# A Hymba layer on one core: the second token block's first weight pair and three of its token factors kept in DRAM instead of being divided again

## The chip, the core and the metric

The program runs on one core of a Trainium2 chip. The metric is the device time of one execution in microseconds (us), lower is better. In single precision each operand of a product is divided into a high part (rounded to the matmul's format) and a low part (the rest), and three matmuls, high by high, high by low and low by high, stand for one product. This division, called a split below, is what the change is about.

## The reference, cut to what matters

```python
def swiglu(h, w_gate, w_up, w_down):
    a = jax.nn.silu(jnp.einsum('bld,df->blf', h, w_gate)) * jnp.einsum('bld,df->blf', h, w_up)
    return jnp.einsum('blf,fd->bld', a, w_down)

def reference(x, meta_tokens, ...):
    h = layer_norm(jnp.concatenate([meta, x], axis=1), ln_in_g, ln_in_b)
    for l in range(DEPTH):                    # DEPTH = 1
        mix = hybrid_mixer(h, ...)            # sliding-window attention beside gated linear attention
        h = layer_norm(ALPHA * h + mix, ln1_g[l], ln1_b[l])
        ffn = swiglu(h, w_ffn_gate[l], w_ffn_up[l], w_ffn_down[l])
        h = layer_norm(ALPHA * h + ffn, ln2_g[l], ln2_b[l])
    return h[:, N_META:]
```

2048 tokens, width 1024, hidden width 2816, float32. The change lies in `swiglu`, in the two products with the gate and up weights.

## The kernel before

The mixer stands in the first part of the span; the first gate product follows at about 965 us, the down product at about 1822 us.

**Gate and up.** The tokens are cut into two blocks of 1024 (`tb` 0 and 1), the 2816 hidden columns into eleven pairs of 256 (`p` 0 to 10). For each block and pair the 2 by 2 by 2 block product is done with seven products in place of eight (Strassen's scheme in Winograd's form). In the order of the program they are named after their token factor: b11, t2, t1, b21, t3, t4, b22. b11, b21 and b22 are plain quarters of the tokens (a quarter is 512 rows of the width by 512 tokens), t1 to t4 are sums and differences of quarters, kept in DRAM as `t_sc`. The weight factors are, in the same order, pa11, ps2, ps1, pa12, ps3, pa22, ps4: pa are plain quarters of the weights, ps sums and differences. A product is two halves of twelve matmuls, 128x128 by 512 columns: four slices of the width (k 0 to 3), three matmuls each.

**Token factors** are made once for a block (`make`): a quarter comes from DRAM in four rows of 256 KB (`r_b`, `r_t`, in a ring of four buffers, tag `cb`), and `split_into` writes the high part on ScalarE (ACT) and the low part on VectorE (DVE) or GpSimd (POOL) in turn (`h_b`, `h_t`). In the last pair of block 0 the code calls `make` for block 1 behind each product, since each factor has one buffer, which comes free with that product.

**Weight factors** are made anew for each pair and block (`weights`): four quarters of 512 KB are fetched about a pair ahead (`fetch_weights`, tiles `a11` to `a22`), POOL forms three of the sums and differences in `s1`, `a21`, `a11` and a fourth in `a12`, ACT writes the seven high parts, POOL four of the low parts (pa11, ps2, pa12, pa22) and DVE three (ps1, ps3, ps4). The divided factors (high and low, 1 MB) stand in a ring of four buffers, tag `whl`; the buffer of a factor comes free when the product four places earlier is done.

**Behind the products** DVE adds the seven results to the quarters of gate and up (`u`, `p`, `c`), ACT takes a tanh, DVE finishes the gates (`sa`, `sb`), POOL forms the factors of the down product (`sc`, `s4`), and seven stores of 256 KB a pair take them to DRAM (`a_sc`, `a_last`).

**What sets the order.** Each engine runs its instructions in the order in which the program was built; the builder's scheduler sets it from priorities and its own estimate of times, but what is marked `held` keeps the order in which it was written among its like. All loads and stores here go through one queue, that of SyncE (SP), in program order: an instruction there that waits for a buffer holds up everything behind it. DMA completions are counted on eight semaphores taken in turn, so that an issue also waits for the DMA eight places before it.

Of the kernel before, what the change touches and what calls it, by code (L numbers as in the profile page):

```python
# [20 lines left out]
NP = NF // 2  # L21
# [102 lines left out]
def body(ctx, tc, t, seq):  # L124
    nc = tc.nc
    NSB = seq // TB
    PSUM = bass.MemoryType.PSUM
    r32 = lambda ap: ap.bitcast(F32)

    cp = ctx.enter_context(tc.tile_pool(name="cp", bufs=1))  # L130
    dr = ctx.enter_context(tc.tile_pool(name="dr", bufs=1, space=bass.MemoryType.DRAM))
# [4 lines left out]
    HT = TF // 2  # L136
    NTB = seq // TF
# [46 lines left out]
    def split_into(hi, lo, src, lo_eng=None, hold=lambda i: i):  # L184
        hold(nc.scalar.activation(hi, src, AF.Copy))  # L185
        hold((lo_eng or nc.vector).tensor_tensor(lo, src, r32(hi), op=ALU.subtract))  # L186
# [547 lines left out]
    pools = {}  # L734

    def quarter(tb, kh, th, k, n):

        c = tb * TF + th * HT
        k0 = kh * (KT // 2) + k
        return n_scT[c // TB][:, k0 : k0 + n, c % TB : c % TB + HT]  # L740
# [37 lines left out]
        yield  # L778

    SOURCE = {"b11": (0, 0), "b21": (1, 0), "b22": (1, 1)}  # L780
    COMBINED = {"t2": (0, 0), "t1": (0, 1), "t4": (1, 0), "t3": (1, 1)}

    def make(f, tb):

        if f in FIRST:
            x = hb.tile([P, 2, KT // 2, HT], F32R, tag="h16", name=f"h_{f}_{tb}", bufs=2)
        else:
            pool = pools["hop1" if f in EARLY else "hop3" if f == "b22" else "hop2"]
            x = pool.tile([P, 2, KT // 2, HT], F32R, tag=f"h_{f}", name=f"h_{f}_{tb}", bufs=1)
        if f in FIRST and tb == 0:  # L790
            for k in range(0, KT // 2, 2):
                raw = staging(f"r_{f}{tb}_{k}").rearrange("p (k q) -> p k q", q=HT)
                if f in SOURCE:
                    nc.sync.dma_start(raw, quarter(tb, *SOURCE[f], k, 2))
                else:
                    i, j = COMBINED[f]
                    nc.sync.dma_start(raw, t_sc[tb][i, :, k : k + 2, j])
                split_into(x[:, 0, k : k + 2], x[:, 1, k : k + 2], raw, nc.vector)
            return x
        for k in range(KT // 2):  # L800
            if tb > 0:
                raw = pools["hop4"].tile([P, HT], F32, tag="cb", name=f"r_{f}{tb}_{k}", bufs=4)
            else:
                raw = pools["hop1"].tile([P, HT], F32, tag="mk", name=f"r_{f}{tb}_{k}", bufs=3)
            if f in SOURCE:
                row_ = nc.sync.dma_start(raw, quarter(tb, *SOURCE[f], k, 1)[:, 0, :])
            else:
                i, j = COMBINED[f]
                row_ = nc.sync.dma_start(raw, t_sc[tb][i, :, k, j])
            if tb > 0:  # L810
                tc.keep_in_program_order(row_)
            split_into(x[:, 0, k], x[:, 1, k], raw, nc.vector if k % 2 else nc.gpsimd)
        return x
# [695 lines left out]

    hops2 = ctx.enter_context(ExitStack())  # L1510
    c2 = ctx.enter_context(ExitStack())
    quarters = {}

    def fetch_weights(p, tb):

        raw = quarters[tb, p] = {}
        pool, tag = (pools["hop4"], "x3") if (tb * NP + p) % 2 else (fp, "x2")
        for a, (i, j) in (("a11", (0, 0)), ("a21", (1, 0)), ("a22", (1, 1)), ("a12", (0, 1))):
            raw[a] = pool.tile([P, D], F32, tag=tag, name=f"{a}_{tb}_{p}", bufs=4)
            nc.sync.dma_start(raw[a], t["w_gu"][p, i, j])  # L1520

    def weights(p, tb):
        nm = f"{tb}_{p}"
        if (tb, p) not in quarters:
            fetch_weights(p, tb)
        raw = quarters.pop((tb, p))
        a11, a12, a21, a22 = (raw[a] for a in ("a11", "a12", "a21", "a22"))

        def parts(x, name, eng=None):
            hl = wpool.tile([P, 2, D], F32R, tag="whl", name=f"{name}_{nm}", bufs=4)  # L1530
            split_into(hl[:, 0, :], hl[:, 1, :], x, eng or nc.gpsimd)
            return hl

        sub = lambda o, x, y: nc.gpsimd.tensor_tensor(o, x, y, op=ALU.subtract)  # L1534
# [3 lines left out]
        nc.gpsimd.tensor_tensor(s1, a21, a22, op=ALU.add)  # L1538
# [25 lines left out]
    def finish_mixing(f):  # L1564
# [8 lines left out]
        ops.update({f: make(f, 0) for f in ("t3", "t4", "b22")})  # L1573
        pools["hop4"] = hops1.enter_context(tc.tile_pool(name="hop4", bufs=1, reuse_waits="tile"))

    for tb in range(NTB):
        for p in range(NP):
            nm = f"{tb}_{p}"
            tl = lambda tag, n: [fp.tile([P, HT], F32, tag=tag, name=f"{n}{w}_{nm}", bufs=2) for w in range(2)]
            w = weights(p, tb)  # L1580
# [4 lines left out]
            def product(f):  # L1585
                if (tb, p) == (0, 0) and f in early:
                    banks[0] += 2
                    out = early[f]
                else:
                    hl, out = next(w), []  # L1590
                    for m in range(2):
                        out.append(bank(f"{f}{m}_{nm}"))
                        matmuls(out[m], ffn_terms(hl, ops[f], m))
                if p == NP - 1 and tb + 1 < NTB:
                    ops[f] = make(f, tb + 1)
                if (tb, p) == (0, 0) and f in BEFORE:
# [12 lines left out]
            for o, x in zip(p1, product("b11")):  # L1609
                nc.scalar.activation(o, x, AF.Copy)  # L1610
            add(u2, p1, product("t2"))
            add(u4, u2, product("t1"))
# [16 lines left out]
            c22 = gate(*c22, sb[:, 0])  # L1629
            store(3, c22)  # L1630
            add(u2, u2, product("t4"))
            c21 = gate(*u2, sb[:, 1])
            store(5, c21)
            add(u4, u4, product("b22"))
# [64 lines left out]
```

## Time and profile before

| | |
|---|---|
| median of three runs (lowest to highest) | 2254.31 us (2252.86 to 2256.03) |
| profiled execution | 2253.32 us, of it the span 2251.5 us |
| mean granted TensorE clock | 0.986 |
| bytes moved by DMA | 446.24 MB, mean 198 GB/s |

The span runs from the first to the last instruction of the one profiled execution; a point of time below is counted from its start. Pair 10 of block 0 begins at 1357.5 us and pair 0 of block 1 follows at 1395.6 us; this stretch is called the boundary below. PE is TensorE's matmuls, PEld its weight loads. An answer by stretches shows, for each engine, busy us and in brackets the instructions, then the granted clock, the busy share of the DMA engines and GB/s.

### The profile page before, as it was taken

To read this page: it belongs to the slowest core of one execution; us is meant where nothing else is said; L and a number is where in the kernel's file an instruction comes from. 1 tells how busy PE (TensorE), PEld (TensorE's weight loads), DVE (VectorE), ACT (ScalarE), POOL (GpSimd) and SP (SyncE) were. 2 spreads that over 40 slices of the span, in tenths; PEclk is the share of its full clock that TensorE was granted. 3 is DMA by queue.
4 is the path that set the end of the run, shared out by engine and by line. 5 is a ranking of instruction groups with operands and counts; after the bars stand their busy time and mean duration, and the time that the engine had idled before them with its cause. 6 is when DMAs were issued, how large, how long until landed. Compare 5 with 4: busy or idle time off the path is not lost.

```text
span 2251.5 us, 31598 instructions
## 1 busy us (share of the span) xinstructions
PE 2173.4 (97%) x11540; PEld 1868.7 (83%) x11540; DVE 1504.7 (67%) x2439; ACT 837.7 (37%) x1458; POOL 1243.6 (55%) x968
## 2 busy tenths in 40 slices
PE   7999999899999999899999999999999999999998
PEld 6888889787899989877888888788888888888886
DVE  6655645565855668356899667785656566885787
ACT  6554544434243342343322324332222232222343
POOL 3766645644615243248677767877675634542433
PEclk9999999899999999999999999999999999999999
DMA  9969672664777587862434235333232278675563
GB/s 334 339 224 292 216 259 97 216 229 166 275 256 288 184 306 247 318 206 95 168 136 164 98 113 172 123 127 117 94 109 101 94 264 304 226 251 198 164 231 129
DMA packets 178911, 446.24 MB, mean 198 GB/s; under 512 B 16530, under 2 KB 62515, under 8 KB 166468
## 3 DMA queue, kind: packets, MB, share of 16 engines
q1 hardware_dynamic: 174948, 441.78, 56.4%
q10 hardware_dynamic: 3808, 2.45, 0.3%
q8 instruction: 91, 1.49, 0.3%
q14 instruction: 64, 0.52, 0.1%
HBM read 299.33 MB, written 144.83 MB: 197 GB/s over the span
## 4 chain that ended last, share of the span: by engine, by line
PE 81%; DVE 7%; DMA 4%; issue 3%; POOL 3%; ACT 2%; SPq 0%; DVEq 0%; ACTq 0%; POOLq 0%
PE d L1347 18%; PE t L197 18%; PE b L197 13%; PE pu L197 13%; PE po L197 6%; PE pv L197 4%; PE oa L667 2%; PE lp L1126 2%; DVE xq L1120 1%; DMA mS_sc<-ms 1%; PE s L614 1%; PE s L615 1%; POOL a L1534 1%; PE pt L655 1%; POOL pa L186 1%
## 5 line engine op out<-in xcount | busy, mean ns | idle before, releaser
L1347 PE MATMUL d<-B,A 128*128 128x512 f32 x1848 | 419.0, 389 | 0.0
L1347 PEld LDWEIGHTS d<-B,A 128*128 128x128 f32 x1848 | 347.0, 188 | 71.9
L197 PE MATMUL t<-h_t,ps 128*128 128x512 f32 x1584 | 368.7, 390 | 2.5 <-ACT ps L185 2.5
L197 PEld LDWEIGHTS t<-h_t,ps 128*128 128x128 f32 x1584 | 297.5, 188 | 64.5 <-ACT ps L185 3.1
L197 PE MATMUL pu<-h,hl_u 128*128 128x512 f32 (+1 forms) x1008 | 247.5, 392 | 8.0 <-ACT h L185 4.3
L197 PE MATMUL b<-h_b,pa 128*128 128x512 f32 x1032 | 244.6, 392 | 3.1 <-POOL pa L186 3.1
L197 PEld LDWEIGHTS b<-h_b,pa 128*128 128x128 f32 x1032 | 195.2, 189 | 45.1 <-POOL pa L186 4.4
L186 POOL TENSOR_TENSOR pa<-a,pa 128x1024 fp32r<-128x1024 f32 x65 | 170.2, 2621 | 92.3 <-ACT pa L185 92.3
L197 PEld LDWEIGHTS pu<-h,hl_u 128*128 128x128 f32 x1008 | 181.7, 194 | 40.8 <-ACT h L185 6.4
L197 PE MATMUL po<-hl_o,msh 128*128 128x256 f32 x1024 | 201.3, 291 | 6.9 <-DVE yo L906 6.1
L186 DVE TENSOR_TENSOR A<-rA,A 128x1024 fp32r<-128x1024 f32 (+1 forms) x78 | 120.1, 1565 | 98.3 <-ACT A L185 98.3
L197 PEld LDWEIGHTS po<-hl_o,msh 128*128 128x128 f32 x1024 | 163.8, 193 | 8.9 <-DVE yo L906 8.1
L185 ACT ACTIVATE A<-rA 128x1024 fp32r<-128x1024 f32 (+1 forms) x78 | 78.6, 1042 | 214.4 <-PE d L1347 183.3
L197 PE MATMUL po<-hl_o,msl 128*128 128x256 f32 x512 | 148.1, 289 | 0.0
L1602 DVE TENSOR_TENSOR u<-u,t 128x512 f32<-128x512 f32 x132 | 89.4, 680 | 76.6 <-PE t L197 76.4
L197 PE MATMUL b<-h_b,ps 128*128 128x512 f32 x528 | 125.8, 393 | 2.5 <-ACT h_b L185 1.8
L197 PE MATMUL t<-h_t,pa 128*128 128x512 f32 x528 | 124.3, 390 | 2.7 <-POOL pa L186 2.7
L1534 POOL TENSOR_TENSOR a<-a,a 128x1024 f32<-128x1024 f32 x44 | 124.5, 2829 | 1.6
L197 PEld LDWEIGHTS b<-h_b,ps 128*128 128x128 f32 x528 | 99.8, 190 | 24.7 <-ACT h_b L185 2.2
L197 PEld LDWEIGHTS t<-h_t,pa 128*128 128x128 f32 x528 | 98.9, 188 | 23.9 <-POOL pa L186 3.6
L197 PE MATMUL pv<-hl_vg,gh 128*128 128x256 f32 (+1 forms) x768 | 110.8, 300 | 5.4 <-DVE vg L1012 4.6
L185 ACT ACTIVATE ps<-a 128x1024 fp32r<-128x1024 f32 x66 | 69.8, 1058 | 121.0 <-PE t L197 76.3
(353 smaller groups left out, 4331.1 us busy)
## 6 DMA issues: line engine op xcount, KB each, us to landing
a<-w_gu SPq DMA_DIRECT2D x88, 512.0 KB, 4.4
hl_u<-w_u SPq DMA_DIRECT2D x42, 1024.0 KB, 6.2
rA<-a_sc SPq DMA_DIRECT2D x66, 512.0 KB, 5.0
w<-w_d SPq DMA_DIRECT2D x50, 512.0 KB, 5.0
hl_o<-w_o SPq DMA_DIRECT2D x24, 1024.0 KB, 6.8
hT_sc<-h SPq DMA_DIRECT2D x32, 512.0 KB, 6.4
gh<-hT_sc SPq DMA_DIRECT2D x16, 1024.0 KB, 10.0
w_u<-hl_u SPq DMA_DIRECT2D x14, 1024.0 KB, 8.4
```

The source lines that it names most:

```text
L185: hold(nc.scalar.activation(hi, src, AF.Copy))
L186: hold((lo_eng or nc.vector).tensor_tensor(lo, src, r32(hi), op=ALU.subtract))
L197: nc.tensor.matmul(out, l, r, start=(i == 0), stop=(i == n - 1))
L614: nc.tensor.matmul(sp[:, :272], q, khh[:, hh, w], start=True, stop=False)
L615: nc.tensor.matmul(sp[:, :272], q, kll[:, hh, w], start=False, stop=True)
L655: nc.tensor.transpose(tp[:, x, :], pr[:, n, 2 * (x % 2) + x // 2, NM:144], ident)
L667: nc.tensor.matmul(oa[:, n], l, m, start=False, stop=(hh == 1 and i == 5))
L1120: nc.vector.tensor_tensor(x[rows[hh], :, hh, :].rearrange("p j (b c) -> p j b c", c=c), eq[rows[hh]], qv[rows[hh], :, :, 1, :], op=ALU.mult)
L1126: nc.tensor.matmul(o[:, P * j : P * j + P], kl[:, j, :], x[:, j].rearrange("p h q -> p (h q)"), start=True, stop=True)
L1347: nc.tensor.matmul(pt, a_[:, a, ca], fb[:, b, cb], start=(p == 0 and j == 0), stop=(p == NP - 1 and j == 2))
L1534: sub = lambda o, x, y: nc.gpsimd.tensor_tensor(o, x, y, op=ALU.subtract)
L1602: nc.vector.tensor_tensor(o[i], x[i], y[i], op=ALU.add)
```

## The change

Three things are changed.

1. In block 0, pair 1 (`KEPT`) stores its seven divided weight factors to DRAM (`parts_sc`, 1 MB each). Block 1 begins with this pair (`ORDER`: 1, 0, 2, 3, ..., 10) and loads the seven factors straight into the ring `whl`; its raw weights are neither fetched nor divided.
2. In pairs 6 to 9 of block 0 (a thirteenth call falls into pair 10) `quarters_later` takes the twelve rows of b11, b21 and b22 of block 1 one by one: load, high part on ACT, low part on DVE in place, two stores to DRAM (`f_sc`). The calls stand behind the products t2, b21 and t4.
3. `make` for these three factors in block 1 is then two loads of 1 MB, without a split. t1 to t4 are made as before.

```diff
     SOURCE = {"b11": (0, 0), "b21": (1, 0), "b22": (1, 1)}
+    f_sc = {f: dr.tile([P, 2, KT // 2, HT], F32, name=f"f_sc_{f}") for f in SOURCE}
+    def quarters_later(tb):
+        rows = [(f, k) for f in SOURCE for k in range(KT // 2)]
+        raw = {}
+        def load(j):
+            f, k = rows[j]
+            raw[j] = pools["hop4"].tile([P, HT], F32, tag="cb", name=f"q_{f}{tb}_{k}", bufs=4)
+            held(nc.sync.dma_start(raw[j], quarter(tb, *SOURCE[f], k, 1)[:, 0, :]))
+        load(0)
+        yield
+        for j, (f, k) in enumerate(rows):
+            if j + 1 < len(rows):
+                load(j + 1)
+            hi = pools["hop1"].tile([P, HT], F32R, tag="mk", name=f"hi_{f}{tb}_{k}", bufs=3)
+            x = raw.pop(j)
+            held(nc.scalar.activation(hi, x, AF.Copy))
+            held(nc.vector.tensor_tensor(x.bitcast(F32R), x, r32(hi), op=ALU.subtract))
+            for a, part in enumerate((r32(hi), x)):
+                nc.sync.dma_start(f_sc[f][:, a, k, :], part)
+            yield
...
+        if tb > 0 and f in SOURCE:
+            for k in range(0, KT // 2, 2):
+                held(nc.sync.dma_start(r32(x)[:, :, k : k + 2, :], f_sc[f][:, :, k : k + 2, :]))
             return x
...
     def weights(p, tb):
         nm = f"{tb}_{p}"
+        if tb > 0 and p == KEPT:
+            for x in parts_sc:
+                hl = wpool.tile([P, 2, D], F32R, tag="whl", name=f"{x}_{nm}", bufs=4)
+                nc.sync.dma_start(r32(hl), parts_sc[x])
+                yield hl
+            return
...
             split_into(hl[:, 0, :], hl[:, 1, :], x, eng or nc.gpsimd)
+            if p == KEPT and NTB > 1:
+                parts_sc[name] = dr.tile([P, 2, D], F32, name=f"parts_{name}")
+                nc.sync.dma_start(parts_sc[name], r32(hl))
             return hl
...
+    KEPT = 1
+    ORDER = [(tb, p) for tb in range(NTB) for p in (range(NP) if tb == 0 else [KEPT] + [p for p in range(NP) if p != KEPT])]
     for tb in range(NTB):
-        for p in range(NP):
+        for p in [p for x, p in ORDER if x == tb]:
...
+            def later():
+                if tb == 0 and NTB > 1 and p >= 2 + KT // 2:
+                    next(later_, None)
...
-            if p + 1 < NP:
-                fetch_weights(p + 1, tb)
-            elif tb + 1 < NTB:
-                fetch_weights(0, tb + 1)
+            nxt = ORDER.index((tb, p)) + 1
+            if nxt < len(ORDER) and (ORDER[nxt][0] == 0 or ORDER[nxt][1] != KEPT):
+                fetch_weights(*ORDER[nxt])
```

The diff doesn't tell the order on the engines, so three places of it follow. In the names the first number behind an underscore is the block and the second the pair (`pa12_1_0` is pa12 of block 1, pair 0; `h_t3_1`, a token factor, has the block alone); the last number is the builder's.

POOL at the boundary, before, from the split of t1 on; pair 0 of block 1 is the pair that is needed next:

```order
L186 TENSOR_TENSOR ps2_1_0_13857<-a11_1_0_13632,ps2_1_0_13857 128x1024
L186 TENSOR_TENSOR h_b21_1_13613<-r_b211_0_13614,h_b21_1_13613 128x512
L186 TENSOR_TENSOR h_b21_1_13613<-r_b211_2_13622,h_b21_1_13613 128x512
L1538 TENSOR_TENSOR s1_1_1_14089<-a21_1_1_13952,a22_1_1_13954 128x1024
L186 TENSOR_TENSOR h_t3_1_13674<-r_t31_0_13675,h_t3_1_13674 128x512
L1534 TENSOR_TENSOR a21_1_1_13952<-a11_1_1_13950,a21_1_1_13952 128x1024
L186 TENSOR_TENSOR pa12_1_0_13919<-a12_1_0_13638,pa12_1_0_13919 128x1024
L1642 TENSOR_TENSOR sc_0_10_13806<-sa_0_10_13640,sb_0_10_13697 128x512
L186 TENSOR_TENSOR h_t3_1_13674<-r_t31_2_13683,h_t3_1_13674 128x512
L186 TENSOR_TENSOR h_t4_1_13732<-r_t41_0_13733,h_t4_1_13732 128x512
```

And now, from the split of t1 on; here pair 1 of block 1 is needed next and pair 0 after it:

```order
L186 TENSOR_TENSOR h_t1_1_13652<-r_t11_2_13661,h_t1_1_13652 128x512
L1690 TENSOR_TENSOR sc_0_10_13857<-sa_0_10_13705,sb_0_10_13762 128x512
L1692 TENSOR_TENSOR sc_0_10_13857<-sc_0_10_13857,sa_0_10_13705 128x512
L1694 TENSOR_TENSOR sa_0_10_13705<-sa_0_10_13705 128x512
L1696 TENSOR_TENSOR s4_0_10_13525<-sb_0_10_13762,sc_0_10_13857 128x512
L186 TENSOR_TENSOR h_t3_1_13739<-r_t31_0_13740,h_t3_1_13739 128x512
L186 TENSOR_TENSOR h_t3_1_13739<-r_t31_2_13748,h_t3_1_13739 128x512
L186 TENSOR_TENSOR pa11_1_0_14129<-a11_1_0_13993,pa11_1_0_14129 128x1024
L186 TENSOR_TENSOR h_t4_1_13797<-r_t41_0_13798,h_t4_1_13797 128x512
L1573 TENSOR_TENSOR a11_1_0_13993<-s1_1_0_14128,a11_1_0_13993 128x1024
```

The weight work of the pair that comes next, and the splits of b11, b21 and b22, are gone from POOL; the first weight factor it makes here belongs to the pair after that.

SP's queue before, in the same stretch: loads of rows of 256 KB, each behind a buffer of the ring `cb`.

```order
L806 DMA r_b211_3_13626<-n_scT2_64 128x512
L1581 DMA a_sc5_10_133<-sb_0_10_13697 128x512
L809 DMA r_t31_0_13675<-t_sc1_67 128x512
L809 DMA r_t31_1_13679<-t_sc1_67 128x512
L809 DMA r_t31_2_13683<-t_sc1_67 128x512
L809 DMA r_t31_3_13687<-t_sc1_67 128x512
```

SP's queue now, from the load of ps1 on; rows of 128x2048 and 128x2x1024 are 1 MB each.

```order
L1557 DMA ps1_1_1_13933<-parts_ps1_11045 128x2048
L1623 DMA a_sc5_10_133<-sb_0_10_13762 128x512
L838 DMA r_t11_3_13665<-t_sc1_67 128x512
L827 DMA h_b21_1_13700<-f_sc_b21_4436 128x2x1024 x2
L827 DMA h_b22_1_13849<-f_sc_b22_4437 128x2x1024
L838 DMA r_t31_0_13740<-t_sc1_67 128x512
L838 DMA r_t31_1_13744<-t_sc1_67 128x512
L827 DMA h_b22_1_13849<-f_sc_b22_4437 128x2x1024
L838 DMA r_t31_2_13748<-t_sc1_67 128x512
L1557 DMA pa12_1_1_13963<-parts_pa12_11078 128x2048
L1623 DMA a_sc4_10_122<-sc_0_10_13857 128x512
L1623 DMA a_sc1_10_89<-sc_0_10_13857 128x512
```

Both halves of the factor b22, which the last product of the new pair reads, now stand ahead of pa12, which its fourth product reads.

PE's order changes in one place, in pair 1 of block 1 behind product t3. Before, pair 0 of block 1 ran its products whole, one behind the other; now matmuls of the next pair's b11 and of b22 stand between those of t4:

```order
L197 MATMUL b110_1_0_14132<-h_b11_1_13562,pa11_1_0_14129 128x512 x2
L197 MATMUL b111_1_0_14145<-h_b11_1_13562,pa11_1_0_14129 128x512 x2
L197 MATMUL t40_1_1_14047<-h_t4_1_13797,pa22_1_1_14045 128x512
L197 MATMUL t41_1_1_14060<-h_t4_1_13797,pa22_1_1_14045 128x512
L197 MATMUL b110_1_0_14132<-h_b11_1_13562,pa11_1_0_14129 128x512 x10
L197 MATMUL b111_1_0_14145<-h_b11_1_13562,pa11_1_0_14129 128x512
L197 MATMUL t40_1_1_14047<-h_t4_1_13797,pa22_1_1_14045 128x512 x5
L197 MATMUL t41_1_1_14060<-h_t4_1_13797,pa22_1_1_14045 128x512 x5
```

Where before one product followed the other, the third and fourth slices of t4 now come 27 matmuls behind the end of t3, fifteen of them from the next pair's b11.

More of the change, by code (lines that the diff above doesn't have):

```diff
@@ L798, in make @@
                 split_into(x[:, 0, k : k + 2], x[:, 1, k : k + 2], raw, nc.vector)
+            return x
+        if tb > 0 and f in SOURCE:
+            for k in range(0, KT // 2, 2):
+                held(nc.sync.dma_start(r32(x)[:, :, k : k + 2, :], f_sc[f][:, :, k : k + 2, :]))
             return x
@@ L1511, in body, with fetch_weights @@
     c2 = ctx.enter_context(ExitStack())
-    quarters = {}
-    def fetch_weights(p, tb):
+    quarters, parts_sc = {}, {}
+    later_ = quarters_later(1)
+    def fetch_weights(tb, p):
         raw = quarters[tb, p] = {}
-        pool, tag = (pools["hop4"], "x3") if (tb * NP + p) % 2 else (fp, "x2")
+        pool, tag = (pools["hop4"], "x3") if ORDER.index((tb, p)) % 2 else (fp, "x2")
         for a, (i, j) in (("a11", (0, 0)), ("a21", (1, 0)), ("a22", (1, 1)), ("a12", (0, 1))):
@@ L1523, in weights @@
         nm = f"{tb}_{p}"
+        if tb > 0 and p == KEPT:
[4 more added lines that the diff above has]
+            return
         if (tb, p) not in quarters:
-            fetch_weights(p, tb)
+            fetch_weights(tb, p)
         raw = quarters.pop((tb, p))
@@ L1611, in body @@
             add(u2, p1, product("t2"))
+            later()
             add(u4, u2, product("t1"))
             add(p1, p1, product("b21"))
-            if p + 1 < NP:
-                fetch_weights(p + 1, tb)
-            elif tb + 1 < NTB:
-                fetch_weights(0, tb + 1)
+            later()
+            nxt = ORDER.index((tb, p)) + 1
+            if nxt < len(ORDER) and (ORDER[nxt][0] == 0 or ORDER[nxt][1] != KEPT):
+                fetch_weights(*ORDER[nxt])
             if (tb, p) == (NTB - 1, NP - 1):
@@ L1631, in body @@
             add(u2, u2, product("t4"))
+            later()
             c21 = gate(*u2, sb[:, 1])
```

## The prediction

> **What bounds the kernel now.** I read the engines' shares and the chain on the page first, then what TensorE waits for in the stretch that the change touches, then TensorE's own rows there.
>
> ```profile
> PE 2173.4 (97%) x11540; PEld 1868.7 (83%) x11540; DVE 1504.7 (67%) x2439; ACT 837.7 (37%) x1458; POOL 1243.6 (55%) x968
> PE 81%; DVE 7%; DMA 4%; issue 3%; POOL 3%; ACT 2%; SPq 0%; DVEq 0%; ACTq 0%; POOLq 0%
> ```
>
> TensorE is busy for 97% of the span, so a gain can only come from its gaps. The change removes no matmul. In the timeline of PE (start, us, and in brackets the idle time before) the product b21 stands at the same place of every pair, and so measures a pair:
>
> ```profile
> 1335.77 5.60 PE L197 MATMUL b<-h_b,pa 128*128 128x512 f32 x24
> ...
> 1357.53 5.60 PE L197 MATMUL b<-h_b,pa 128*128 128x512 f32 x24
> ...
> 1373.85 5.60 PE L197 MATMUL b<-h_b,pa 128*128 128x512 f32 x24
> ...
> 1414.65 6.92 PE L197 MATMUL b<-h_b,pa 128*128 128x512 f32 x22 [2.11 <-POOL pa L186]
> ...
> 1429.68 5.29 PE L197 MATMUL t<-h_t,pa 128*128 128x512 f32 x22 [2.21 <-POOL pa L186]
> ...
> 1468.89 5.28 PE L197 MATMUL t<-h_t,pa 128*128 128x512 f32 x22 [0.52 <-POOL pa L186]
> ```
> ```profile
> 1495.77 5.60 PE L197 MATMUL b<-h_b,pa 128*128 128x512 f32 x24
> ...
> 1533.85 5.60 PE L197 MATMUL b<-h_b,pa 128*128 128x512 f32 x24
> ```
>
> From 1335.77 to 1373.85 and from 1495.77 to 1533.85 a pair takes 38.08 us: no gap there. From 1373.85 to 1495.77 three pairs take 121.92 us, 7.68 more than three times 38.08. **These 7.7 us are all that the boundary can give.** Three waits make 4.84 of it, all for POOL's low part of a weight factor (pa12 and pa22). The stretches around them show the rest (PE, PEld, DVE, ACT, POOL busy, granted clock, DMA share, GB/s):
>
> ```profile
> 1405.00:1415.00 10.00, 7.89 (x36) 6.22 (x35) 9.96 (x6) 4.45 (x7) 10.00 (x5) 1.00 0.33 107
> 1415.00:1425.00 10.00, 10.00 (x38) 8.11 (x37) 6.94 (x7) 4.91 (x7) 10.00 (x6) 0.83 0.55 173
> 1425.00:1435.00 10.00, 7.79 (x34) 6.12 (x33) 6.29 (x6) 4.42 (x6) 10.00 (x7) 1.00 0.74 272
> ```
>
> POOL is full throughout. Behind the first wait the granted clock is 0.83 over 10 us, 1.7 us of lost matmul time; around the second, of the same length, it is 1.00. The remaining 1.1 us stands in no row as a wait.
>
> **What goes.** POOL's work from 1372 to 1440 us by groups (count, busy us, mean ns):
>
> ```profile
> L186 POOL TENSOR_TENSOR pa<-a,pa 128x1024 fp32r<-128x1024 f32 x5 | 13.8, 2751 | 0.0
> L186 POOL TENSOR_TENSOR h_b<-r_b,h_b 128x512 fp32r<-128x512 f32 x6 | 10.2, 1697 | 8.0 <-ACT h_b L185 8.0
> L1534 POOL TENSOR_TENSOR a<-s,a 128x1024 f32<-128x1024 f32 x2 | 5.7, 2843 | 0.1
> L1534 POOL TENSOR_TENSOR a<-a,a 128x1024 f32<-128x1024 f32 x2 | 5.2, 2622 | 0.0
> L1538 POOL TENSOR_TENSOR s<-a,a 128x1024 f32<-128x1024 f32 x1 | 2.9, 2862 | 0.0
> L186 POOL TENSOR_TENSOR ps<-a,ps 128x1024 fp32r<-128x1024 f32 x1 | 2.4, 2396 | 0.0
> ```
>
> The six `h_b` splits go, 10.2 us. One whole pair's weight work goes too: three low parts `pa` 8.3, one `ps` 2.4, one sum 2.9, three differences 8.1 (2.8 + 2 x 2.6), 21.7 us. That is 31.9 us of work against 4.8 us of waits, and by the order what POOL does first here serves the pair after the kept one. I expect no wait for a low part of a weight at the boundary: minus 7.7. ACT and DVE lose splits too, off the path.
>
> **What comes at the boundary: bytes.** The pair that was divided is now loaded. Rates: the two stretches say what the DMA engines move when they always have work, and what they move here now; the third line is the 40 slices of 455 to 485 us, where loads of 1 MB queue up.
>
> ```profile
> 460.00:480.00 20.00, 17.21 (x91) 13.82 (x90) 13.67 (x42) 8.22 (x13) 8.86 (x19) 0.91 1.01 404
> 1372.00:1440.00 68.00, 63.67 (x272) 51.89 (x271) 52.64 (x48) 30.46 (x45) 58.92 (x30) 0.97 0.58 193
> ```
> ```profile
> GB/s 240 289 382 421 448 415 426 415 426 415 393 339 426 426 437 388 404 426 404 388 399 410 421 415 426 410 399 415 415 408 391 405 366 166 39 22 0 0 0 0
> ```
> ```profile
> r_t<-t_sc SPq DMA_DIRECT2D x16, 256.0 KB, 3.0
> ```
>
> The upper bound is 426 GB/s; the lower 193 at a share of 0.58, 333 if the share were full. I take 404, nearest because it too is loads of 1 MB in a queue: 2.6 us per MiB. A lone load of 256 KB takes 3.0 us of which 0.65 is moving; I count 1.5 us ahead of the bytes and 0.5 behind.
>
> Now the queue, by the order shown. A product is 38.08 / 7 = 5.44 us. Pair 10 begins at 1357.53, so its t4 ends at 1390.2, its b22 at 1395.6, and the kept pair wants pa12 (its product b21) at 1395.6 + 3 x 5.44 = 1411.9. The load of ps1 waits for t4 of pair 10 (its buffer in the ring of four); ahead of it stands the last kept row, which waits for DVE behind the first half of t4. So the queue cannot run full before about 1391, its bytes not before 1392.5. From there to the end of pa12 it holds four rows of t1 (1 MiB), ps1 (1), a store (0.25), b21 (2), b22 (2), three rows of t3 (0.75) and pa12 (1): 8.0 MiB, 20.8 us. pa12 is there at 1392.5 + 20.8 + 0.5 = 1413.8: **TensorE waits 1.9 us for it**. At 426 GB/s it is 0.8, at 333 (3.15 us per MiB) 6.3. A wait of that size may halve the clock for a while as the one at 1414.65 did: of the two like it one did, so 0.85 us, half of 1.7. New cost at the boundary: 2.8 us.
>
> The Trainium skill, TensorE: Matmul & The Clock Gate, section Part 1: The HAM clock gate, has the clock halved after at least one idle window of about 3.4 us; by that a wait of 1.9 us would cost no clock and the sum would be 0.85 us better. The row of 0.83 behind a wait of 2.11 us speaks against it.
>
> The later deadlines follow in the same way. Up to the last row of t4 the queue holds 5.25 MiB more (stores 1, ps3, pa22, ps4, five rows 1.25): 13.25 MiB, 34.5 us, there at 1427.5, split by about 1429.6. t3 ends at 1413.8 + 2 x 5.44 = 1424.7; by the order 27 matmuls of 5.44 / 24 us, 6.1 us, follow before the later slices of t4 are read, at 1430.8. No second wait, with 1 us to spare. There also stands a new dependence: the last slice of t4 is split on DVE behind the gates of t3 of the same pair, which those 27 matmuls cover.
>
> **What comes earlier.** Pair 1 stores 7 MiB and pairs 6 to 9 carry twelve rows (0.75 MiB, one ACT and one DVE split each).
>
> ```profile
> 1020.00:1060.00 40.00, 40.00 (x172) 32.98 (x171) 29.32 (x26) 12.14 (x15) 35.59 (x16) 0.96 0.30 100
> 1258.00:1296.00 38.00, 38.00 (x169) 31.48 (x168) 24.05 (x25) 10.94 (x13) 26.09 (x13) 1.00 0.30 107
> ```
> ```profile
> w_o<-hl_o SPq DMA_DIRECT2D x8, 1024.0 KB, 4.9
> ```
> ```profile
> L185 ACT ACTIVATE h_b<-r_b 128x512 fp32r<-128x512 f32 x5 | 3.2, 633 | 8.6 <-DMA r_b<-n_scT 8.5
> ```
> ```profile
> L186 DVE TENSOR_TENSOR h_t<-r_t,h_t x8: 680/1478/2876, 1385.8 to 1420.8; 128x512 fp32r<-128x512 f32 x8
> ```
>
> In 40 us around pair 1 the DMA engines are free 70% of the time, room for 0.7 x 40 us x 404 GB/s = 11.3 MB; the stores bring 7.3. A divided factor's buffer is now free only when its store has landed, 4.9 us for such a store, while the ring leaves four products, 21.8 us. In a pair of 38 us with three rows DVE is busy 24 us and gets 2.0 to 8.6 more (three times 0.68 to 2.88), ACT 11 and gets 1.9, the DMA engines 0.30 and get 2.4 MB, 5.8 us. I cost both at nothing, covered by the dense products of these pairs. If a cover fails I bound it by one store behind time, 0 to 4.9 us, and take 0, since TensorE waits for nothing in either stretch. Below nothing is excluded: a pair without a gap cannot get faster.
>
> **Sum.** Against the profiled execution, 2253.32 us: minus 7.7, plus 2.8, 2248.4. The median of the runs is 1.0 above that execution, so the forecast for a median is **2249.4 us**, 0.22% faster. About 0.2%, 4.5 us, is what a measurement of this kernel can tell from no change, so the forecast sits on that edge.
>
> **Rivals.**
> 1. *No new wait.* If the queue fills a little earlier, or moves 426 GB/s, the wait for pa12 is below 1 us and costs no clock: 2254.3 - 7.7 = 2246.6, or 2247.4 with 0.8. For it: the slices of 415 to 426. Against it: two loads of b22, 2 MiB not needed before the last product, stand ahead of pa12.
> 2. *The transfer takes POOL's place.* At 333 GB/s the wait is 6.3 us, with the halved clock 8.0, and the result 2254.6: no change. For it: 193 GB/s at a share of 0.58 in this very stretch, and stores among the loads. Against it: that row counts loads of 256 KB that found the queue empty, not a full queue. The Trainium skill, DMA: Bandwidth & Descriptors, section Specifications, puts the HBM limit of one core at about 358 GB/s; by that the wait would be 4.5 us and the time about 2252.5. The rows of 404 to 426 GB/s, loads from the same DRAM, speak against the limit here.
> 3. *Slower.* The same stream, at the kept pair's fourth product, with reads and writes of DRAM mixed at a lower rate still: the boundary loses as much as before when pa12 comes 6.0 us late (with 1.7 of clock), at 338 GB/s, and it ends 4.5 us slower when pa12 comes 10.5 us late, at 1422.4, (1422.4 - 0.5 - 1392.5) / 8 = 3.67 us per MiB, 285 GB/s. That is 2258.8. For it: no stretch before has 8 MiB back to back beside gates and stores. Against it: 285 is under both bounds.
> 4. *The change does not free TensorE:* the splits of t4 come late because DVE and ACT take the gates of t3 first, beyond the 6.1 us of cover. A slip of 3 us gives 2252.4, inside rival 2's reach.
>
> **Chances.** The forecast, a wait of 1 to 4 us at pa12 and 2247.5 to 2252.5, gets 0.53; rival 1 0.15; rivals 2 and 4 together 0.20; rival 3 0.12. Faster by over 0.2% is under 2249.8: rival 1 and some 0.30 of the forecast, 0.45. Slower by over 0.2% is rival 3, 0.12. The rest, 0.43, is within 0.2%. The range reaches from just under rival 1, 2246.0, to past rival 2 and a part of the earlier costs, 2256.0, and leaves out most of rival 3.
>
> **What would show it.** Right: in the stretch from the kept pair on, no row of PE waits for POOL's `pa`; the b21 product waits one to three us for a DMA (the parts of pa12), or for nothing; the DMA share is 0.9 or more from the end of pair 10 for some 20 us; three pairs from there take about 117 us instead of 121.9; the pairs 1 and 6 to 9 keep 38.08 us. Wrong: a wait for `h_t` of t4 or for ps3 and pa22; a DMA share under 0.8 while PE waits for a load, which would mean that the queue's order and not its rate holds pa12 back; or gaps in pair 1 or 2, where the stores are.

## The result, and the profile after

| | before | with the change |
|---|---|---|
| median (lowest to highest), six runs each | 2253.59 us (2247.38 to 2256.03) | 2279.57 us (2273.33 to 2282.26) |
| profiled execution, of it the span | 2253.32, 2251.5 us | 2278.53, 2276.7 us |
| ratio to before | | 1.012, interval 1.0099 to 1.0141 |

The kernel is 1.2% slower. The forecast was 2249.4 us, 0.2% faster, with a range up to 2256.0: the time lies outside it, on the other side. First the page of the changed kernel, its engines' shares and the head of its chain, beside which those of before stand in the prediction:

```profile
PE 2181.8 (96%) x11540; PEld 1870.7 (82%) x11540; DVE 1500.5 (66%) x2442; ACT 828.3 (36%) x1451; POOL 1216.0 (53%) x954
PE 40%; DVE 9%; DMA 5%; issue 5%; POOL 4%; ACT 2%; SPq 1%; DVEq 0%; ACTq 0%; POOLq 0%
```

POOL has 27.6 us less to do, as was meant, and DVE and ACT less too; yet the share of PE in the chain falls from 81% to 40%. Work has gone and waits have come. The timeline of PE (start, us, and in brackets the idle time before) shows where:

```profile
1045.35 5.60 PE L197 MATMUL b<-h_b,pa 128*128 128x512 f32 x24
...
1197.67 5.60 PE L197 MATMUL b<-h_b,pa 128*128 128x512 f32 x24
...
1254.62 5.30 PE L197 MATMUL b<-h_b,pa 128*128 128x512 f32 x22 [1.94 <-POOL pa L186]
...
1297.65 6.90 PE L197 MATMUL b<-h_b,pa 128*128 128x512 f32 x22 [2.32 <-POOL pa L186]
...
1341.54 6.88 PE L197 MATMUL b<-h_b,pa 128*128 128x512 f32 x22 [2.32 <-POOL pa L186]
...
1364.58 5.60 PE L197 MATMUL b<-h_b,pa 128*128 128x512 f32 x24
...
1408.28 8.44 PE L197 MATMUL b<-h_b,pa 128*128 128x512 f32 x24 [5.46 <-issue]
...
1439.87 8.03 PE L197 MATMUL b<-h_b,pa 128*128 128x512 f32 x24 [9.34 <-DMA pa<-parts_pa]
...
1502.13 5.60 PE L197 MATMUL b<-h_b,pa 128*128 128x512 f32 x24
```

The rows at 1045.35, 1197.67 and 1364.58 us begin pairs 2, 6 and 10; the row at 1502.13 begins the third pair of block 1. Four pairs from 1045.35 take 152.32 us, four times 38.08: dense. From 1197.67 to 1364.58, pairs 6 to 9, it is 166.91, **14.6 us lost** where before nothing was lost: there pair 6 began at 1205.21, 152.32 us ahead of pair 10 at 1357.53.

```profile
1205.21 5.60 PE L197 MATMUL b<-h_b,pa 128*128 128x512 f32 x24
```

From 1364.58 three pairs take 137.55, **23.3 lost at the boundary** where before it was 7.7. The account of the 25.2 us between the two profiled executions: plus 14.6, plus 15.6, minus 7.5 by which pair 2 began earlier (1045.35 against 1052.89), and plus 2.5 behind the boundary. The 7.5 is not put down to the change: in the eleven other changed kernels below the profiled execution began pair 2 between 1041.3 and 1048.9 us, with and without pair 1's stores, and why it varies was not followed.

**Why the rows cost.** POOL's low part `pa` is late in pairs 7, 8 and 9, though POOL is far from full. Follow the first late row back. The timeline of SP (DMA issues), at the end of a pair and in the middle of the next:

```profile
1214.92 0.32 SPq L1623 DMA_DIRECT2D a_last<-s  x1
1215.29 2.34 SPq L792 DMA_DIRECT2D q_b<-n_scT  x2
...
1240.07 0.32 SPq L1623 DMA_DIRECT2D a_sc<-sb  x1
1240.45 0.41 SPq L792 DMA_DIRECT2D q_b<-n_scT  x1
```

And the timelines of ACT, of DVE and of POOL:

```profile
1223.00 0.63 ACT L801 ACTIVATE hi_b<-q_b 128x512 fp32r<-128x512 f32 x1 [13.14 <-DMA q_b<-n_scT]
...
1243.59 0.63 ACT L801 ACTIVATE hi_b<-q_b 128x512 fp32r<-128x512 f32 x1 [2.28 <-DMA q_b<-n_scT]
```
```profile
1224.61 1.23 DVE L186 TENSOR_TENSOR ps<-a,ps 128x1024 fp32r<-128x1024 f32 x1 [9.74 <-ACT ps L185]
```
```profile
1228.45 2.39 POOL L186 TENSOR_TENSOR pa<-a,pa 128x1024 fp32r<-128x1024 f32 x1 [11.21 <-ACT pa L185]
...
1246.58 2.41 POOL L1577 TENSOR_TENSOR s<-a,a 128x1024 f32<-128x1024 f32 x1 [7.08 <-DVE ps L186]
...
1251.77 2.79 POOL L186 TENSOR_TENSOR pa<-a,pa 128x1024 fp32r<-128x1024 f32 x1
```

A row's load (`q_b`) stands on SP behind the last store of a pair (`a_last`), which waits until POOL has computed `s`. ACT takes its instructions in order; it stands 13.1 us at the row's high part (5.4 until the load is issued, 7.7 until it lands), and the splits of the next pair's weights stand behind it. POOL waits 11.2 us for one of these splits, DVE 9.7 us for another. POOL's wait is not the one that reaches PE, for POOL is idle twice more before pa12. DVE's is: the gates behind it are late, so the store of a gate (`a_sc`) goes out late, at 1240.07, and the next row's load stands behind that store. ACT waits 2.3 us more for this row, its next split is late, POOL waits 7.1 us for DVE's half of it, and the low part of the next pair's pa12 ends at 1251.77 + 2.79 = 1254.56. PE, which wanted it at 1252.7, begins at 1254.62. POOL's late work makes the next `a_last` late, at 1264.48, and behind it stand the next loads. The chain of releases in the next pair, as the profile follows it back (start, us, what), goes through both loads again:

```profile
1264.48 0.32 SPq L1623
...
1264.86 3.82 DMA q_b<-n_scT
...
1268.75 1.24 ACT hi_b L801 x2
...
1281.10 2.03 DVE sb L1591
...
1283.51 3.04 DMA q_b<-n_scT
...
1288.31 1.24 DVE ps L186
...
1294.81 2.79 POOL pa L186
```

**It is a loop:** POOL, store, load, ACT, DVE's gates, store, load, ACT, DVE, POOL. Two more stores `a_last` were issued at 1307.47 and 1351.35: the loop takes 43.0 and 43.9 us where a dense pair takes 38.08. What either of the two loads would cost alone was not tried.

### The profile page after: what moved, and what is told of

The parts are those of the page before. It is cut to its first block, busy times and chain, and to the rows that moved or that the text cites. A ratio compares the mean times of both kernels' runs of the same rounds, so it can differ in the third digit from the quotient of the medians.

```text
span 2276.7 us, 31638 instructions
## 1 busy us (share of the span) xinstructions
PE 2181.8 (96%) x11540; PEld 1870.7 (82%) x11540; DVE 1500.5 (66%) x2442; ACT 828.3 (36%) x1451; POOL 1216.0 (53%) x954
## 4 chain that ended last, share of the span: by engine, by line
PE 40%; DVE 9%; DMA 5%; issue 5%; POOL 4%; ACT 2%; SPq 1%; DVEq 0%; ACTq 0%; POOLq 0%
PE d L1376 15%; PE t L197 12%; PE b L197 9%; PE po L197 3%; DMA q_b<-n_scT 1%; DVE sa L1591 1%; DMA r_t<-t_sc 1%; DVE u L1648 1%; DVE y L1282 1%; POOL sa L1694 1%; DVE A L186 1%; DVE sb L1591 1%; POOL sc L1690 1%; DMA cb<-n_scT 1%; DMA pa<-parts_pa 1%
## 5 line engine op out<-in xcount | busy, mean ns | idle before, releaser
L197 PE MATMUL b<-h_b,pa 128*128 128x512 f32 x1032 | 251.7, 400 | 22.6 <-DMA pa<-parts_pa 9.3
L186 POOL TENSOR_TENSOR pa<-a,pa 128x1024 fp32r<-128x1024 f32 x62 | 159.0, 2565 | 119.7 <-ACT pa L185 119.7
L1573 POOL TENSOR_TENSOR a<-a,a 128x1024 f32<-128x1024 f32 x42 | 117.5, 2799 | 1.5
L186 DVE TENSOR_TENSOR ps<-a,ps 128x1024 fp32r<-128x1024 f32 x42 | 81.6, 1943 | 44.9 <-ACT ps L185 44.9
```

What stands on the lines that cost most here:

```text
L197: nc.tensor.matmul(out, l, r, start=(i == 0), stop=(i == n - 1))
```

## The experiments

In all kernels pairs 6 to 9 and the boundary are measured as above: four and three pairs, less 38.08 us each.

| run | pairs 6 to 9 lose | boundary loses | median | ratio to before (interval) |
|---|---|---|---|---|
| before | 0.0 | 7.7 | | |
| the change | 14.6 | 23.3 | 2279.57 | 1.0120 (1.0099 to 1.0141) |
| rows_only | 13.2 | 22.2 | 2276.24 | 1.0112 (1.0095 to 1.0130) |
| weights_only | 0.0 | 9.7 | 2250.78 | 1.0005 (0.9994 to 1.0017) |
| rows_ahead | 0.8 | 18.5 | 2259.12 | 1.0040 (1.0022 to 1.0057) |
| rows_on_act_queue | 0.0 | 11.4 | 2250.16 | 1.0006 (0.9992 to 1.0021) |
| b21_early | 0.0 | 1.7 | 2242.26 | 0.9962 (0.9945 to 0.9979) |
| b22_late | 0.0 | 1.4 | 2241.60 | 0.9955 (0.9940 to 0.9970) |
| b21_early_b22_late | 0.0 | 0.0 | 2243.30 | 0.9963 (0.9948 to 0.9978) |
| b21_early_b22_after_pa12 | 0.0 | 0.7 | 2243.13 | 0.9961 (0.9944 to 0.9977) |
| quarters_act_queue | 0.0 | 12.8 | 2251.71 | 1.0025 (1.0007 to 1.0043) |
| quarters_act_b21_early | 0.0 | 3.1 | 2241.61 | 0.9970 (0.9952 to 0.9989) |
| sp_rows_b21_early_b22_late | 13.8 | 10.5 | 2262.84 | 1.0065 (1.0045 to 1.0084) |

The kernel before ran beside each group: medians of 2248.85 us (the four runs of the first group), 2250.68 (the second) and 2248.56 (the last three). The lost times are from one profiled execution of each.

### The change in two halves

**rows_only**, the weights divided as before:

```diff
-    ORDER = [(tb, p) for tb in range(NTB) for p in (range(NP) if tb == 0 else [KEPT] + [p for p in range(NP) if p != KEPT])]
+    ORDER = [(tb, p) for tb in range(NTB) for p in range(NP)]
...
-        if tb > 0 and p == KEPT:
+        if False:
...
-            if p == KEPT and NTB > 1:
+            if False:
...
-            if nxt < len(ORDER) and (ORDER[nxt][0] == 0 or ORDER[nxt][1] != KEPT):
+            if nxt < len(ORDER):
```

> Only the row part of the change: pairs 6 to 9 divide and store the rows, the second block loads the divided factors, but it begins with pair 0 and every weight is divided as before. Theory A (a loop through queues: a row's load stands on SP behind the last store of a pair, which waits for POOL; ACT waits for the row, POOL's low parts wait for ACT, and the loop takes some 43.5 us where a dense pair takes 38.1): pairs 7 to 9 lose about 14.6 us as in the changed kernel, the median is 2266 to 2276. Theory B (the kept weights and their bytes cause the late POOL work too): pairs 7 to 9 lose under 3 us and the median is under 2260.

**weights_only**, the three plain factors loaded and split as before:

```diff
-                if tb == 0 and NTB > 1 and p >= 2 + KT // 2:
+                if False:
                     next(later_, None)
...
-        if tb > 0 and f in SOURCE:
+        if False:
             for k in range(0, KT // 2, 2):
```

> Only the weight part of the change: pair 1's seven divided weights are stored and read back for the first pair of the second block; the quarters are loaded raw and split there as before. Theory A: pairs 1 to 10 all take 38.08 us, and the boundary, with its queue not late, loses 2 to 12 us (before 7.7, with the change 23.3): median 2247 to 2258. Theory B (the bytes of the kept weights are what the boundary pays): the boundary still loses 18 us or more, median over 2263.

The rows alone make nearly the whole loss: 13.2 us in pairs 6 to 9 and, which was not expected, 22.2 at the boundary; the median is 0.2 us over the span that theory A gave. The kept weights alone lose nothing in the pairs (so the seven stores in pair 1 are free) and 9.7 at the boundary, 2 more than before, inside the 2 to 12 of theory A; theory B is out. PE's waits at that boundary (us in total, times, longest) have no low part of a weight among them any more:

```profile
PE b L197 <- POOL h_b L186: 2.5, 1, 2.5
PE b L197 <- DVE h_b L186: 1.9, 1, 1.9
PE t L197 <- DMA pa<-parts_pa: 0.9, 1, 0.9
PE t L197 <- DMA ps<-parts_ps: 0.8, 1, 0.8
```

The splits of b22, which this kernel still makes, come late now, and some loads: one wait has taken the place of the other.

### Is it the wait or the work?

**rows_ahead**, the loads three rows ahead, on the same queue:

```diff
-        load(0)
+        for j in range(3):
+            load(j)
         yield
         for j, (f, k) in enumerate(rows):
-            if j + 1 < len(rows):
-                load(j + 1)
+            if j + 3 < len(rows):
+                load(j + 3)
```

> The whole change, but each row's load is issued three rows ahead of its use instead of one; ACT, DVE and POOL do the same work, the bytes are the same. Theory A: ACT's waits of 8 to 9 us for a row vanish after the first row, pairs 7 to 9 lose under 3 us instead of 14.6; if the late queue at the boundary was a consequence, the boundary falls from 23.3 to about 10 and the median is about 2253, if the bytes alone make it, 23.3 stays and the median is about 2265. Rival (the rows cost by their work on ACT and DVE, not by a wait): pairs 7 to 9 still lose over 10 us, median over 2274.

**rows_on_act_queue**, one row ahead as in the change, but issued by ACT:

```diff
-            held(nc.sync.dma_start(raw[j], quarter(tb, *SOURCE[f], k, 1)[:, 0, :]))
+            held(nc.scalar.dma_start(raw[j], quarter(tb, *SOURCE[f], k, 1)[:, 0, :]))
```

> The whole change, but the rows are loaded from ACT's own DMA queue, one row ahead as in the change, so that no load stands behind a store of SP. Theory A: as with rows_ahead, ACT waits under 2 us for a row, pairs 7 to 9 lose under 3 us, median 2252 to 2266. Rival (not the place in SP's queue but one row of lead is too short, since a row takes 2.7 to 6.4 us to land): ACT still waits over 4 us for rows and pairs 7 to 9 still lose over 8 us, median over 2272.

ACT, DVE and POOL do the same work in the same sizes, and the same bytes move. ACT's waits for a row from 1190 to 1350 us, with the change, and then with the rows on ACT's queue (total, times, longest):

```profile
ACT hi_b L801 <- DMA q_b<-n_scT: 37.1, 6, 13.1
```
```profile
ACT hi_b L801 <- DMA q_b<-n_scT: 0.9, 1, 0.9
```

The loss in the pairs is gone with the waits, 14.6 to 0.0, and the ratio falls from 1.0120 to 1.0006, some 26 us; the median of 2250.16 lies 1.8 us under the span that was expected. Theory A is shown for the pairs, since two kernels that take the wait away by different means lose nothing or 0.8 there. Both rivals are out: the work itself, and that one row of lead is too short. The stretches of one pair say the same (PE, PEld, DVE, ACT, POOL busy, clock, DMA share, GB/s), with the change and with the rows on ACT's queue:

```profile
1273.83:1311.91 38.08, 35.16 (x147) 28.10 (x146) 28.23 (x26) 9.31 (x12) 25.30 (x12) 0.96 0.41 126
```
```profile
1270.20:1308.28 38.08, 38.08 (x169) 31.53 (x168) 28.41 (x29) 12.43 (x17) 27.00 (x13) 1.00 0.49 168
```

DVE, ACT and POOL are as busy or busier in the kernel without a gap. The Trainium skill, DMA: Bandwidth & Descriptors, section Issuing engines are not separate DMA queues, holds that spreading DMAs over issuing engines saves only the time that issuing takes, since all run on the same 16 DMA engines. Here the rate is not what the move changed: the load no longer stands behind a store that waits for POOL. Issuing these twelve loads took SP 0.4 to 1.3 us each; 26 us are more than that, so the sentence does not hold where the issuing engine has waits of its own in the way.

rows_ahead loses 0.8 in the pairs (its first row still waits 11.8 us, no later one does), but 18.5 at the boundary: its median lies between the two numbers of the expectation. So a part of the boundary's loss is lateness that the rows leave behind. SP shows it too: the last store of pair 9, behind which the kept pair's loads stand, was issued at 1389.29 us with the change, 13.4 before the kept pair's start; with the rows on ACT's queue at 1359.64, 24.8 before:

```profile
1389.29 0.32 SPq L1623 DMA_DIRECT2D a_last<-s  x1
...
1395.09 0.51 SPq L1557 DMA_DIRECT2D pa<-parts_pa  x1
```
```profile
1359.64 0.32 SPq L1623 DMA_DIRECT2D a_last<-s  x1
...
1368.31 0.33 SPq L1557 DMA_DIRECT2D pa<-parts_pa  x1
```

(The kept pair's dense start is 1364.58 + 38.08 = 1402.66, and 1384.44.) With 11.4 us less lead the kept pa11, issued at 1395.09, landed 13.1 us later at 1408.2, and PE waited the 5.46 us that its row puts down to "issue".

### What the boundary still loses

With the rows out of the way the boundary loses 11.4 us, all at one place, in PE's timeline:

```profile
1384.44 5.60 PE L197 MATMUL b<-h_b,pa 128*128 128x512 f32 x24
1409.47 8.32 PE L197 MATMUL b<-h_b,pa 128*128 128x512 f32 x24 [8.55 <-DMA pa<-parts_pa]
...
1472.03 5.60 PE L197 MATMUL b<-h_b,pa 128*128 128x512 f32 x24
```

8.55 us of waiting for the kept pa12 and 2.7 at a lower clock behind it (8.32 for 24 matmuls instead of 5.60). SP's timeline shows what stands ahead of pa12: beside a gate store and four rows of 256 KB (not shown) four loads of `h_b` of 1 MB, two for b21 and one for b22 from 1386.43 on, and b22's second at 1393.69:

```profile
1384.80 0.38 SPq L1557 DMA_DIRECT2D ps<-parts_ps  x1
...
1386.43 2.60 SPq L827 DMA_DIRECT2D h_b<-f_sc_b  x3
...
1393.69 0.52 SPq L827 DMA_DIRECT2D h_b<-f_sc_b  x1
...
1394.91 0.42 SPq L1557 DMA_DIRECT2D pa<-parts_pa  x1
```

Four kernels change the places of these loads alone, all with the rows on ACT's queue. **b21_early**: the loads are no longer kept in program order.

```diff
-                held(nc.sync.dma_start(r32(x)[:, :, k : k + 2, :], f_sc[f][:, :, k : k + 2, :]))
+                nc.sync.dma_start(r32(x)[:, :, k : k + 2, :], f_sc[f][:, :, k : k + 2, :])
```

> As rows_on_act_queue, but the loads of the divided factors need not keep the program's order in SP's queue: by the order b21's 2 MiB now stand ahead of pa11, some 17 us earlier, and b22's 2 MiB still stand ahead of pa12. Theory C (pa12 is late by the bytes ahead of it: the queue runs full only from the pair's start, 8 MiB at 2.6 us per MiB and a slow first piece, and landed 24.9 us after the start where TensorE wanted it at 16.3): 2 MiB less is 5.2 us less, the wait for pa12 falls from 8.6 to about 3.4 us, the boundary's loss from 11.4 to about 5, ratio to before about 0.998. Rival D (pa12's place behind gate stores that wait for DVE and POOL holds it, not bytes): the wait stays over 6 us, ratio 1.000 or more.

**b22_late**: b22's loads are put by and asked for where the kept weights load ps3.

```diff
-                held(nc.sync.dma_start(r32(x)[:, :, k : k + 2, :], f_sc[f][:, :, k : k + 2, :]))
+                go = lambda k=k: held(nc.sync.dma_start(r32(x)[:, :, k : k + 2, :], f_sc[f][:, :, k : k + 2, :]))
+                waiting.append(go) if f == "b22" else go()
...
             for x in parts_sc:
+                while x == "ps3" and waiting:
+                    waiting.pop(0)()
```

> As rows_on_act_queue, but b22's loads are asked for later in the program; by the order they stand behind ps4 and the rows of t4, after the first gate store of the kept pair, and b21's stay where they were. Theory C: pa12 comes 5.2 us sooner, wait about 3.4 us; the same bytes then end at the pair's last product, where b22 is wanted 32.6 us after the start and lands at about 39: with the waits before it a second wait of 1 to 4 us; the boundary loses 6 to 9 us, ratio 0.998 to 1.000. Rival D: pa12's wait stays over 6 us and the second comes on top, ratio over 1.001.

**b21_early_b22_late** has both edits (`held` for b22 alone), **b21_early_b22_after_pa12** has both with no `held` at all.

> Both moves: b21's loads ahead of pa11, b22's behind ps4. Theory C: 4 MiB less stand ahead of pa12, it lands about 14.6 us after the start, before TensorE wants it at 16.3: no wait there; b22, last, lands at about 34 and is wanted at 32.6: 0 to 3 us. The boundary loses 1 to 4 us (before 7.7), ratio 0.996 to 0.998: faster than both kernels. Rival D: pa12 still over 6 us late, ratio 1.000 or more.

> b21's loads ahead of pa11, b22's right behind pa12 and so ahead of ps3. Theory C: no wait for pa12, but 2 MiB now stand ahead of ps3, which lands at about 25 us where TensorE wants it at 21.8: a wait of 2 to 4 us moves from pa12 to ps3, the boundary loses 3 to 6 us, ratio 0.997 to 0.999. Rival (order behind pa12 does not matter, all of it comes in time): no wait at ps3 either, the same time as b21_early_b22_late.

PE waited for pa12 until 25.0 us after the kept pair's start in rows_on_act_queue; 1409.49 less 1391.62, 17.9, in b21_early; 1401.63 less 1384.30, 17.3, in b22_late. Their rows:

```profile
1391.62 5.60 PE L197 MATMUL b<-h_b,pa 128*128 128x512 f32 x24
1409.49 5.75 PE L197 MATMUL b<-h_b,pa 128*128 128x512 f32 x24 [1.39 <-DMA pa<-parts_pa]
```
```profile
1384.30 5.60 PE L197 MATMUL b<-h_b,pa 128*128 128x512 f32 x24
1401.63 5.71 PE L197 MATMUL b<-h_b,pa 128*128 128x512 f32 x24 [0.85 <-DMA pa<-parts_pa]
```

With both moves PE's timeline has no gap from one pair to the third after it, 1461.85 less 1347.61 being exactly three times 38.08:

```profile
1347.61 5.60 PE L197 MATMUL b<-h_b,pa 128*128 128x512 f32 x24
...
1461.85 5.60 PE L197 MATMUL b<-h_b,pa 128*128 128x512 f32 x24
```

So theory C holds in kind, the bytes ahead of pa12 made it late, and rival D is out. Its sizes were too cautious: 2 MiB taken from ahead of pa12 were worth 7.1 and 7.7 us where 5.2 were expected, and the second wait that it expected for b22 did not come, so b22_late lost 1.4 us where 6 to 9 were forecast. With b22 right behind pa12 the forecast wait of 2 to 4 us for ps3 was 0.41: there the rival, that the order behind pa12 does not matter, was nearer. All four are faster than the kernel before, by 0.37 to 0.45%, and so than the change; their intervals don't tell them apart.

### Which part pays, and are the parts independent?

> The row part of the change alone, with the rows loaded from ACT's queue: the second block begins with pair 0 and every weight is divided as before; no kept weights. Which part of the change pays? Theory E (the quarters alone free POOL enough: its six splits, 10.2 us, leave the boundary): the boundary loses 0 to 4 us (before 7.7), ratio 0.996 to 0.999, and the kept weights add nothing. Rival F (POOL's weight work for pair 0 still comes late, as in the kernel before): waits for POOL's low parts stay, the boundary loses 5 to 9 us, ratio 0.999 to 1.001.

> As quarters_act_queue, with the divided factors' loads free to move up in SP's queue (b21's 2 MiB some 15 us earlier). Without kept weights no load that the pair needs stands behind them, so theory C says it changes nothing at the boundary: within 2 us of quarters_act_queue there. Rival: the rows of t1 and t3 behind b21 are what sets the boundary, it gains 3 us or more.

> The whole change with the boundary's loads in the better order (b21 ahead of pa11, b22 behind ps4), but the rows again loaded from SP's queue one row ahead, as in the change. Theory A: pairs 7 to 9 lose 12 to 16 us again, as with the change and as rows_only. At the boundary: if the order of the loads was all, it loses under 4 us and the median is about 2257; if the lateness that the rows leave on ACT, DVE and POOL also counts there, it loses 6 to 16 us and the median is 2259 to 2270.

The three are put together from the edits above: the ORDER of rows_only with the rows on ACT's queue; the same without `held`; and b21_early_b22_late with the rows on SP's queue again.

quarters_act_queue was a miss of both theories: 12.8 us, more than before, and PE waits mostly not for weights but for the splits of token factors (`h_t`), whose rows of t3 and t4 stand behind b21 (4.9 us for POOL's splits and 2.2 for DVE's, 1.0 for a `pa`). quarters_act_b21_early was a miss of theory C, which said that b21's place would not matter without kept weights: it gained 9.7 us at the boundary, as much as with them (11.4 to 1.7), as the rival beside it had it. **The place of 2 MiB in the queue is worth more here than either part of the change.** With it, the quarters alone reach 0.9970; the kept weights bring the boundary from 3.1 us to 1.7, too little for these intervals to show.

sp_rows_b21_early_b22_late brings the loop back: 13.8 us in the pairs, and 10.5 at a boundary that lost 0.0 in the same order of loads. There PE waits once, 8.5 us, at the kept pair's first product. The profile puts it down to DVE's sum `u`, which ended at 1407.32 us; but the kept pa11, which the same product reads, was issued at 1395.22 and landed 12.1 us later, at 1407.3 too. So both were late, and which of them alone would have held PE is not shown. The order of the loads is the same in the two kernels; the lateness that the rows leave behind is worth some 10 us at the boundary by itself.

## Why the prediction was wrong, step by step

- **The step that failed** is the one on what comes earlier: "I cost both at nothing, covered by the dense products of these pairs", with "one store behind time, 0 to 4.9 us" as its bound. Half of it was right, pair 1's stores cost nothing. The rows cost 14.6 us where they stand and 11.9 more at the boundary (23.3 against 11.4). The step added up busy time, and busy time was free indeed. It did not ask behind what each new instruction would stand: the load on SP behind a store that waits for POOL, the high part on ACT ahead of the next pair's splits. The order of both engines is fixed when the program is built, so the chain could have been looked for before the run. In place of a cost of nothing stood a loop through the queues of 43.0 to 43.9 us per pair. 14.6 and 11.9 are 26.5 us, which agrees with the distance between the ratios 1.0120 and 1.0006, some 26 us.
- **The term for the bytes** was right in its mechanism and too small: 1.9 us of wait for pa12 and 0.85 of clock were forecast. With the rows' waits gone, in rows_on_act_queue, it was 8.55 and 2.7. The load of ps1 was issued 0.4 us after the kept pair's start, where the bytes were forecast to flow from 3.1 us ahead of it; from there to the end of pa12 it took 24.6 us where 20.8 and 0.5 were forecast; and the clock cost more than the whole 1.7 of which half was taken. While PE waited for pa12 the DMA share was 1.04, with the change and in rows_on_act_queue, so the sign named for an order that holds pa12 back, a share under 0.8, did not come.
- **Minus 7.7 for POOL's waits** was right: no kernel with kept weights waits for a low part of a weight at the boundary. The view of before said that; it could not say what would be late next.
- **No second wait, t4 in time:** right by the runs with the rows on ACT's queue.
- **The forecast's sum** for the change as it was thought, 2249.4 us, and the 2250.2 of rows_on_act_queue are near each other by chance in part: that kernel lost 11.4 at the boundary where the sum had 2.8, and the kernel before was 2248.85 beside it instead of the 2254.31 on which the sum stood.
- **The rivals:** the one on the other side had a late pa12 as its mechanism, at 2258.8. With the change PE did wait 9.34 us for pa12, but that was half of the story of the boundary and no part of that of the pairs. The range left most of this rival out, and no rival had a cost in pairs 6 to 9. The sign that failed first is among those for being right, that the pairs 6 to 9 keep 38.08 us; the gaps that were named for being wrong are those "in pair 1 or 2, where the stores are", and there were no new ones (pair 1 has one wait of 2.6 us where it had one of 2.5). By rival 2's own terms its wait of 4.5 us comes to 2252.8 us with the halved clock, not 2252.5; nothing hangs on it.

## What to carry to other kernels

Free time on an engine hides new work only if the new instruction is ready when its turn comes: for each one that is added, name what stands ahead of it in its queue and what that waits for, on the queue that issues its load too, and look whether the chain closes into a loop. A load that must be early belongs on a queue without waits of its own, or far enough ahead. Where a burst of loads meets a deadline, sort it by the time at which each is needed before thinking of rates.

## What the runs showed of the hardware beyond that

Whether a wait of two microseconds costs clock is not told by its length. With the change 22 matmuls took 5.30 us behind a wait of 1.94 and 6.90 behind 2.32; in the kernel before they took 6.92 behind 2.11 and 5.29 behind 2.21. In rows_only alone both are seen:

```profile
1296.61 5.28 PE L197 MATMUL b<-h_b,pa 128*128 128x512 f32 x22 [2.27 <-POOL pa L186]
...
1340.45 6.85 PE L197 MATMUL b<-h_b,pa 128*128 128x512 f32 x22 [2.33 <-POOL pa L186]
```

The Trainium skill, TensorE: Matmul & The Clock Gate, section Part 1: The HAM clock gate, halves the clock after an idle window of about 3.4 us, and its windows run freely. The waits of 2.1 to 2.3 us are shorter than that and some lost 1.6 us, against the sentence. What decides here is where the wait lies in such a window, and the granted clock shows that. In each of the thirteen traces it is 0.50 or 1.00, and the stretches at 0.50 begin whole multiples of 3.413 us apart. Laid over the span from 1000 to 1800 us, this grid parts the cases: the clock was halved after each of the 28 windows at full clock in which PE was idle for 1.87 us or more (by the profile's modelled busy time), and after none of the 2983 with 1.86 us or less. So an idle window need not be idle as a whole. In rows_only the wait of 2.27 us is cut by a border at 1295.98, and the one of 2.33 lies within one window but for 0.1 us (PE's busy time first, the granted clock behind POOL's):

```profile
1292.57:1295.98 3.41, 1.77 (x8) 1.13 (x6) 3.41 (x2) 1.02 (x2) 3.41 (x2) 1.00 0.00 0
1336.94:1340.35 3.41, 1.18 (x6) 0.64 (x4) 3.41 (x2) 0.47 (x1) 3.41 (x2) 1.00 0.00 0
1340.35:1343.77 3.42, 3.32 (x8) 2.66 (x9) 3.42 (x4) 0.00 (x0) 3.42 (x3) 0.50 0.09 33
```

Two things stay open. The first is what a MiB ahead of pa12 costs. 7.1 and 7.7 us for 2 MiB would be 3.6 to 3.9 us per MiB, but the DMA engines moved 376 GB/s on average over the 25 us of rows_on_act_queue, 2.8 us per MiB. The two moves changed more than 2 MiB: up to the landing of pa12, b21_early's queue ran fuller (412 GB/s over 17.8 us), and b22_late moved 6.3 MB where rows_on_act_queue moved 9.4. That fits the lower price, but was not tried by itself. The second is the time from the third pair of block 1 to the end of the span: it was 772.1 us before and 777.0 to 779.8 in the profiled executions of the four that change the places of the loads beside kept weights. It does not follow the gain, since rows_ahead, which lost 18.5 us at the boundary, has 779.9 there and the rest 772.6 to 776.9. Why it differs was not tried.
